# A decoder layer on one core: the order of the block products in the second MLP product, and where the final norm's row work stands on ScalarE

## The chip, the core and the metric

The kernel runs on one core of a Trainium2 chip, in one launch. The metric is the device time of one execution in microseconds (us), lower is better. The core has a matrix engine (TensorE, in the profile PE for the matmuls and PEld for its weight loads), a vector engine (VectorE, DVE), a scalar engine (ScalarE, ACT), GpSimd (POOL) and a sync engine (SyncE, SP) that here only issues transfers. Each engine works through its own instructions in the order in which they were written, and an instruction that has to wait holds up all that stand behind it on its engine.

## The reference, cut to what matters

The layer is a mixer with two head groups, a cross-attention, a squared-ReLU MLP and a final norm, over 512 tokens of width 1024. The change lies in the last two lines, in the second MLP product (4096 x 1024) and the final norm:

```
x = x + cross_attention(rms_norm(x, norm_xattn), rms_norm(mem, norm_mem), ...)
h = rms_norm(x, norm_mlp)
x = x + jnp.square(jax.nn.relu(h @ w_ff1)) @ w_ff2
return rms_norm(x, norm_final)

def rms_norm(x, g):
    y = x * lax.rsqrt(jnp.mean(x * x, axis=-1, keepdims=True) + NORM_EPS)
    return y * g
```

## The kernel before

Activations lie transposed in SBUF, features on the 128 partitions and tokens along the free axis. All instructions stand in an order written out by hand (`tc.manual_schedule()`), so the order of the Python code is the order on each engine.

**Units.** All weights pass through the kernel in units of 128 x 1024 f32 (512 KB). Unit `u` is loaded by SyncE into a raw tile `wr{u}`, then split into two parts of lower precision that together hold it: ScalarE writes the high part `wh{u}` (`A.activation(..., AF.Copy)` into fp32r), VectorE writes the rest `wl{u}` (`wr - wh`). TensorE then does three matmuls for each block: high x high, high x low, low x high. `need(u)` stands ahead of unit `u`'s matmuls and writes the splits up to unit `u + 2`; there are four buffers for `wh` and three for `wl`, so a split can run only a few units ahead of TensorE.

**The second MLP product.** It is done by block products after Strassen and Winograd: seven products of quarter-size blocks instead of eight. Products 0 to 5 (`p` in the code) are computed "across" (tokens on the partitions) in eight units of 12 matmuls with 512 columns, into the PSUM pairs X, Y or Z; product 6 ends in eight units of 24 matmuls with 256 columns into W. The units of this stage are 124 to 179: position 0 has units 124 to 131, position 1 has 132 to 139, and so on; the last, product 6, has 172 to 179. Each product has four operands `op{i}`, again a high part from ScalarE and a low part from VectorE, made from the tiles `g0` to `g7` (the first MLP product's outcome) or from sums of them that VectorE makes in place (`make_sum`).

**From a product to the output.** When a product is done, its PSUM pair is copied or added to a pair of SBUF tiles `c` (`after_across`). A `turn` then transposes these on TensorE into a PSUM tile `ct`, four small matmuls, and VectorE adds `ct` to the residual `x1[h]` (`x10` and `x11` in the order's rows). Each `turn` has two halves, taken from the list `turns` one at a time behind the units `j = 2` and `j = 3` of a product. `place(h, t, b)` is a quarter of the residual: `h` picks the half of the features, `t` the half of the tokens (256 each).

**Row work.** Where a quarter of the residual is complete (`full`), `norm_part(h, t, n)` does what the final norm needs of row block `n`: on ScalarE a square into `fsq` (or `Sf`, the first time) and a copy scaled by the gain into `xg`, which is a part of the `g` tiles that is no longer needed; on VectorE the addition of the square to the sum `Sf{t}`. When the eight row blocks of a token half `t` are through, `final_half` sums `Sf` and the last square over the partitions with two matmuls (`fs`), ScalarE makes the reciprocal root (`rb`, an Ln and an Exp), VectorE multiplies four pieces of `xg` with it, and SyncE stores each of them.

Before the change, `norm_part` is called right after the addition, in the same place of the program:

```
for h, t, op, full in uses:
    d = place(h, t, b)
    getattr(V, op)(d, d, two(ps))
    if full:
        norm_part(h, t, 2 * b)
        norm_part(h, t, 2 * b + 1)
```

and the products run in the order 0, 1, 2, 3, 4, 5, 6. The quarter (0, 0) needs products 0 and 5 and so gets its addition in the midst of product 6; (1, 0) gets it in product 4, (1, 1) in product 5, (0, 1) in the last units of product 6 (`ends_last`).

Of the kernel before, what the change touches and what calls it, by code (L numbers as in the profile page):

```python
# [32 lines left out]
FF2 = MLP + 7 * 8  # L33
# [89 lines left out]
def hybrid_layer(ctx: ExitStack, tc: tile.TileContext, xT, memT, ws, vecs, consts, rots, out):  # L123
# [21 lines left out]
    def s2(dtype, name, shape=(T,)):  # L145
        if name.startswith(EARLY2):
            return ep.tile([P, *shape], dtype, tag="e2", name=name, bufs=N2E)
        return sp.tile([P, *shape], dtype, tag="s2", name=name, bufs=N2)

    def l8(dtype, name):  # L150

        n8[0] += 1
        if n8[0] % 5 < 2:
            return s8(dtype, name)
        return late[0].tile([P, 4, T], dtype, tag="l8", name=name, bufs=N8L)
# [4 lines left out]
    def acc_bank(name):  # L160
        return pacc.tile([P, T], F32, tag="acc", name=name)

    def side_bank(name):
        return pside.tile([P, T], F32, tag="ps", name=name)
# [21 lines left out]
    def two(ap):  # L186
        return ap.rearrange("p (n c) -> p n c", n=2)

    E, F = ([[f(i, j) for j in range(2)] for i in range(2)] for f in (f1_block, f2_block))
    FT = [[dram.tile([4, P, D], F32, name=f"u{b}_{c}") for c in range(2)] for b in range(4)]  # L190
    FU = [[t[n] for t in row for n in range(4)] for row in FT]

    def f2_across(block):

        return [block[c][:, :, 2 * T // 4 * q:2 * T // 4 * (q + 1)] for c in range(2) for q in range(4)]

    def f2_rows(i, j):

        us = [MLP + 16 * (2 * i + c) + 8 + 4 * j for c in range(2)]
        return [ws[u:u + 4] for u in us]  # L200
    XO = (0, 4, 1, 5, 2, 6, 3, 7)
    sources = [ws[u] for u in range(MLP - 8)] + [ws[MLP - 8 + n] for n in XO] + [None] * (FF2 - MLP)
    LAST = (0, 2, 1, 3)
    for block in (f2_rows(0, 0), FT[0], FT[1], f2_rows(1, 1), FT[2], f2_rows(1, 0)):
        sources += f2_across(block)
    sources += FU[3][:4] + [FU[3][4 + n] for n in LAST]

# [150 lines left out]
    def start(g, key, wait=0.0):  # L358
        rec = [g, None, key]
        made[key] = rec  # L360
        side.append(rec)
        set_wait(rec, wait)
# [35 lines left out]
    def transpose(o, i):  # L398
        PE.transpose(o, i, ident)

    def mm(o, l, r, start, stop):
        last_mm[0] = PE.matmul(o, l, r, start=start, stop=stop, skip_group_check=True)
        since[0] += 1
        if since[0] >= GAP:
            pump()
# [87 lines left out]
    for i in range(2):  # L493
        t = ep.tile([P, NT, P], F32, name=f"AT{i}")
# [6 lines left out]
    def gain(g, k):  # L501
        return vec[:, g * KT + k:g * KT + k + 1]
# [599 lines left out]
    def part(k, h):  # L1102

        return g[k][:, :, h * half:(h + 1) * half]
# [13 lines left out]
    def f1_rest():  # L1118
        while rest:
            rest.pop(0)()  # L1120

    def f1_group(j):
# [36 lines left out]
        for p, ks in steps:  # L1159
# [30 lines left out]
    OPS = [lambda k: part(k, 0), lambda k: part(k, 1), lambda k: part(k, 1), lambda k: part(k, 0),  # L1190
           lambda k: part(k, 1), lambda k: part(k + 4, 0), lambda k: part(k + 4, 1)]

    def make_sum(p, k):

        if p == 2:
            V.tensor_add(part(k, 1), part(k, 1), part(k, 0))
        elif p == 3:
            V.tensor_sub(part(k, 0), part(k, 1), part(k + 4, 0))
        elif p == 4:
            V.tensor_sub(part(k, 1), part(k, 1), part(k + 4, 1))  # L1200

    sum_state = [0]

    def need_sum(i):
        while sum_state[0] < min(28, i + 1):
            make_sum(*divmod(sum_state[0], 4))
            sum_state[0] += 1

    ops = {}
    op_state = [0]  # L1210
    def make_op():

        i = op_state[0]
        op_state[0] += 1
        need_sum(i)
        src = OPS[i // 4](i % 4)
        both = l8(F32R, f"op{i}").rearrange("p a b -> p (a b)")
        hi, lo = (x.rearrange("p (k c) -> p k c", k=4) for x in (both[:, :D], both[:, D:]))
        if i // 4 == 2:
            A.activation(hi, src, AF.Copy, scale=-1.0)  # L1220
            V.scalar_tensor_tensor(lo, src, -1.0, hi.bitcast(F32), op0=ALU.mult, op1=ALU.subtract)
        else:
            A.activation(hi, src, AF.Copy)
            V.tensor_sub(lo, src, hi.bitcast(F32))
        ops[i] = [(hi[:, k], lo[:, k]) for k in range(4)]

    def need_op(i):
        while op_state[0] < min(28, i + 1):
            make_op()
# [7 lines left out]
    def place(h, t, b):  # L1237

        return x1[h][:, 2 * b:2 * b + 2, t * half:(t + 1) * half]
# [5 lines left out]
    def xg(t, a, b):  # L1245

        return part(2 * t + a // 4, 0)[:, a % 4:b - a + a % 4]

    def norm_part(h, t, n):

        f = 4 * h + n
        d = x1[h][:, n, t * half:(t + 1) * half]
        q = Sf[t] if squares[t] == 0 else s2(F32, f"fsq{f}")
        A.activation(q[:, :half], d, AF.Square)
        A.activation(xg(t, f, f + 1), d[:, None, :], AF.Copy, scale=gain(G_FIN, f))
        squares[t] += 1
        if 1 < squares[t] < KT:
            V.tensor_add(Sf[t][:, :half], Sf[t][:, :half], q[:, :half])
        elif squares[t] == KT:
            start(final_half(t, Sf[t], q), ("fin", t))  # L1260

    def final_half(nb, S, q):

        ps = side_bank("fs")
        yield [S[:, :half]]
        smm(ps[:, :half], ones, S[:, :half], True, False)
        yield [q[:, :half]]
        smm(ps[:, :half], ones, q[:, :half], False, True)
        r = rbf[:, nb * half:(nb + 1) * half]
        rsqrt_of(r, ps[:, :half], D)  # L1270
        for eng, a, b in ((V, 0, 2), (V, 2, 4), (V, 4, 7), (V, 7, 8)):
            x = xg(nb, a, b)
            eng.tensor_mul(x, x, r[:, None, :].to_broadcast([P, b - a, half]))
            SY.dma_start(out[nb, :, a:b], x)
# [12 lines left out]
            A.activation(c[m], banks[m], AF.Copy)  # L1287
        return c

    turns = []  # L1290

    def turn(c, uses):

        def one(b):
            ps = side_bank("ct")
            for n in range(2):
                for m in range(2):
                    o = n * half + m * P
                    transpose(ps[:, o:o + P], c[m][:, (2 * b + n) * P:(2 * b + n + 1) * P])
            for h, t, op, full in uses:  # L1300
                d = place(h, t, b)
                getattr(V, op)(d, d, two(ps))
                if full:
                    norm_part(h, t, 2 * b)
                    norm_part(h, t, 2 * b + 1)
        for b in range(2):
            turns.append(lambda b=b: one(b))

# [4 lines left out]
    X, Z = ([acc_bank(f"{x}{b}") for b in range(2)] for x in "XZ")  # L1313
    Y = [side_bank(f"Y{b}") for b in range(2)]
# [18 lines left out]
    def prepare(p, j):  # L1333
        i = 4 * p + j // 2
        need_op(i + 1 + j % 2)
        need_sum(i + 3)

    PLAN = ((X, True), (Y, True), (X, False), (Y, False), (X, False), (Z, True))

    for p, (banks, begins) in enumerate(PLAN):  # L1340
        for j in range(8):
            c, q = j // 4, j % 4
            w = FF2 + 8 * p + j
            need(w)
            f1_rest()
            prepare(p, j)
            hi, lo = (x[w].rearrange("p (n k c) -> p n k c", n=4, k=2) for x in (his, los))
            for kk in range(2):
                a_hi, a_lo = ops[4 * p + j // 2][(2 * j + kk) % 4]
                w_hi, w_lo = hi[:, :, kk], lo[:, :, kk]  # L1350
                for m in range(2):
                    acc = banks[m].rearrange("p (n c) -> p n c", n=4)
                    t_hi, t_lo = a_hi[:, m * P:(m + 1) * P], a_lo[:, m * P:(m + 1) * P]
                    mm(acc, t_hi, w_hi, begins and j == 0 and kk == 0, False)
                    mm(acc, t_hi, w_lo, False, False)
                    mm(acc, t_lo, w_hi, False, j == 7 and kk == 1)
            if j in (2, 3) and turns:
                turns.pop(0)()
        after_across(p)

    X = [acc_bank(f"W{b}") for b in range(2)]
    p = 6
    for j in range(8):
        i, c, n = 8 * p + j, j // 4, j % 4
        if c:
            n = LAST[n]
        need(FF2 + i)
        f1_rest()
        need_op(4 * p + 2 * c + 1 + (0, 1, 2, 2)[j % 4])
        hi, lo = his[FF2 + i], los[FF2 + i]  # L1370
        acc = two(X[n // 2])[:, n % 2]
        for k in range(8):
            a_hi, a_lo = ops[4 * p + 2 * c + k // 4][k % 4]
            w_hi, w_lo = hi[:, k * P:(k + 1) * P], lo[:, k * P:(k + 1) * P]
            mm(acc, w_hi, a_hi, c == 0 and k == 0 and n % 2 == 0, False)
            mm(acc, w_hi, a_lo, False, False)
            mm(acc, w_lo, a_hi, False, c == 1 and k == 7)
        if j in (2, 3):
            turns.pop(0)()
        if c:  # L1380
            ends_last(X, n)
    drain(("fin", 0))
# [76 lines left out]
```

## Time and profile before

| | |
|---|---|
| median of 3 runs | 751.92 us (750.88 to 751.99) |
| the profiled execution's own time | 752.65 us |
| its span, first to last instruction | 750.9 us |
| mean granted TensorE clock | 0.994 |
| busy: PE, DVE, ACT, POOL | 730.4, 546.0, 419.9, 49.5 us |
| the stage of the change, units 124 to 179 | from 576.4 us to 741.6 us of the span |

The span is what the instructions of one profiled execution cover; that execution's own time is 1.75 us longer. A row of the timeline has the start in us from the span's beginning, the duration in us, the engine, the line (here L115 nearly everywhere, a helper that records each operation), the operation, what it writes and reads with the buffers' numbers left out, and how many instructions were merged. In brackets stands how long the engine had been idle before it, and what ended that.

### The profile page before, as it was taken

How to read it: one execution, taken by the hardware profiler on the slowest of the kernel's cores; microseconds unless marked ns; L12 is line 12 of the kernel's file. 1: busy time of each engine (PE TensorE's matmuls, PEld its weight loads, DVE VectorE, ACT ScalarE, POOL GpSimd, SP SyncE). 2: the span in 40 equal slices, each digit the busy share in tenths (PEclk: the TensorE clock that was granted, in tenths of full speed). 3: DMA queues.
4: the chain of work that ended last, by engine and by line, in shares of the span. 5: the costliest groups of instructions: out<-in, count | busy, mean ns of one | idle time of the engine just before them, and what ended most of it. 6: DMA issues, size and time to landing. Idle time of an engine off the chain costs nothing.

```text
span 750.9 us, 10919 instructions
## 1 busy us (share of the span) xinstructions
PE 730.4 (97%) x4152; PEld 635.3 (85%) x4152; DVE 546.0 (73%) x893; ACT 419.9 (56%) x642; POOL 49.5 (7%) x62
## 2 busy tenths in 40 slices
PE   6999999999999999999999999999999999999994
PEld 4888888777777998888888999999999888887793
DVE  5888554877766646666468788787879688877764
ACT  6673347344855554555365755565556556647652
POOL 1000000000011210011001011222100000000000
PEclk9999999999999999999999999999999999999997
DMA  8425334534689897369826498889986765655413
GB/s 276 143 83 168 113 113 136 166 120 141 171 206 245 207 293 283 137 134 273 284 95 142 117 264 212 217 228 217 238 219 209 212 197 183 196 182 169 155 42 112
DMA packets 62868, 136.95 MB, mean 182 GB/s; under 512 B 4544, under 2 KB 31552, under 8 KB 62176
## 3 DMA queue, kind: packets, MB, share of 16 engines
q1 hardware_dynamic: 53376, 110.64, 43.4%
q0 software_dynamic: 8960, 25.17, 18.9%
q8 instruction: 32, 0.52, 0.3%
q10 hardware_dynamic: 480, 0.45, 0.2%
q14 instruction: 20, 0.16, 0.1%
HBM read 134.15 MB, written 35.65 MB: 226 GB/s over the span
## 4 chain that ended last, share of the span: by engine, by line
PE 92%; DVE 3%; ACT 2%; DMA 1%; issue 1%; DVEq 0%; ACTq 0%
PE X L115 21%; PE Y L115 15%; PE xo L115 7%; PE mkq L115 6%; PE xq L115 6%; PE wo L115 5%; PE hg L115 3%; PE mv L115 3%; PE memv L115 3%; PE hq L115 3%; PE hi L115 3%; PE Z L115 3%; PE memk L115 2%; PE W L115 2%; PE hf L115 2%; PE xs L115 2%
## 5 line engine op out<-in xcount | busy, mean ns | idle before, releaser
L115 ACT ACTIVATE wh<-wr 128x1024 fp32r<-128x1024 f32 (+2 forms) x126 | 130.3, 1042 | 111.4 <-PE wo L115 19.6
L115 DVE TENSOR_TENSOR wl<-wr,wh 128x1024 fp32r<-128x1024 f32 (+2 forms) x126 | 151.2, 1204 | 43.9 <-ACT wh L115 34.0
L115 PE MATMUL X<-wh,op 128*128 128x512 f32 x192 | 61.0, 392 | 0.1
L212 POOL DMA_DIRECT2D u<-in_ws_dram x32 | 31.0, 968 | 329.0 <-PE hg L115 201.5
L115 PE MATMUL Y<-OS,wh 128*128 128x256 f32 x256 | 47.2, 284 | 0.2 <-ACT t L115 0.2
L115 PE MATMUL X<-OS,wh 128*128 128x256 f32 x256 | 46.5, 283 | 0.0
L115 PEld LDWEIGHTS X<-wh,op 128*128 128x128 f32 x192 | 36.1, 188 | 7.9 <-ACT wh L115 0.5
L115 PEld LDWEIGHTS Y<-OS,wh 128*128 128x128 f32 x256 | 39.9, 192 | 0.5 <-ACT t L115 0.4
L115 PEld LDWEIGHTS X<-OS,wh 128*128 128x128 f32 x256 | 39.9, 192 | 0.0
L115 PE MATMUL Y<-wh,op 128*128 128x512 f32 x128 | 39.7, 389 | 0.0
L115 PE MATMUL X<-wl,op 128*128 128x512 f32 x96 | 37.5, 391 | 0.8 <-DVE wl L115 0.8
L115 PE MATMUL X<-OS,wl 128*128 128x256 f32 x128 | 36.2, 283 | 0.0
L115 PE MATMUL Y<-OS,wl 128*128 128x256 f32 x128 | 36.2, 283 | 0.0
L115 ACT ACTIVATE g<-t 128x512 f32<-128x512 f32 x32 | 19.0, 625 | 30.5 <-DVE t L115 30.5
L115 ACT ACTIVATE op<-g 128x1024 fp32r<-128x1024 f32 x28 | 29.3, 1046 | 0.5 <-PE X L115 0.5
L115 DVE TENSOR_TENSOR op<-g,op 128x1024 fp32r<-128x1024 f32 x24 | 29.3, 1219 | 0.0
L115 ACT ACT_TABLE_LOAD x22 | 28.2, 1283 | 1.5 <-PEq L1447 1.2
L115 PEld LDWEIGHTS Y<-wh,op 128*128 128x128 f32 x128 | 24.0, 188 | 5.0
L115 PE MATMUL W<-op,wh 128*128 128x256 f32 x128 | 25.1, 296 | 2.3 <-DVE x L115 2.3
L115 PE MATMUL mkq<-xhi,wh 128*128 128x512 f32 x64 | 26.7, 417 | 0.0
L115 PE MATMUL mkq<-xlo,wh 128*128 128x512 f32 x64 | 26.6, 416 | 0.0
L115 PE MATMUL mkq<-xhi,wl 128*128 128x512 f32 x64 | 26.3, 411 | 0.0
(321 smaller groups left out, 2141.1 us busy)
## 6 DMA issues: line engine op xcount, KB each, us to landing
wr<-in_ws_dram SPq DMA_DIRECT2D x90, 512.0 KB, 4.3
u<-in_ws_dram POOLq DMA_DIRECT2D x32, 512.0 KB, 7.5
wr<-u SPq DMA_DIRECT2D x32, 512.0 KB, 4.2
u<-in_ws_dram SPq DMA_DIRECT2D x16, 512.0 KB, 3.5
u<-u SPq DMA_DIRECT2D x16, 512.0 KB, 5.3
wA<-in_ws_dram SPq DMA_DIRECT2D x8, 512.0 KB, 7.1
wD<-in_ws_dram SPq DMA_DIRECT2D x8, 512.0 KB, 6.8
wB<-in_ws_dram SPq DMA_DIRECT2D x8, 512.0 KB, 4.1
```

What stands on the lines that cost most here:

```text
L115: return f(*args, **kw)
L212: return nc.gpsimd.dma_start(dst, src, accum_op=ALU.add, max_dma_last_dim=4 * D)
```

## The change

The products run in the order 0, 5, 1, 2, 3, 4, 6 (`SEQ`): product 5, which used to be sixth, becomes the second. The loads, the operands, the sums and `PLAN` follow that order. `norm_part` is no longer called where the addition is written; a call is put on a list, and `between`, which stands behind each unit, takes two of them off the list before it takes a half of a `turn`. So a row block's ScalarE work stands one unit behind the addition that it reads. The row work of quarter (0, 0) is kept back (`held_rows`) until unit `j = 3` of product 3, which sits at position 4, since it writes into parts of `g0` and `g1` that are operands up to there. In product 6 the halves of the last `turn` stand behind `j = 1` and `j = 2` instead of 2 and 3.

```diff
-    for block in (f2_rows(0, 0), FT[0], FT[1], f2_rows(1, 1), FT[2], f2_rows(1, 0)):
+    for block in (f2_rows(0, 0), f2_rows(1, 0), FT[0], FT[1], f2_rows(1, 1), FT[2]):
...
+    SEQ = (0, 5, 1, 2, 3, 4, 6)
+
+    def make_sum(i):
+
+        p, k = SEQ[i // 4], i % 4
...
-        src = OPS[i // 4](i % 4)
+        p = SEQ[i // 4]
+        src = OPS[p](i % 4)
...
                 if full:
-                    norm_part(h, t, 2 * b)
-                    norm_part(h, t, 2 * b + 1)
+                    rows = held_rows if (h, t) == (0, 0) else norms
+                    for n in (2 * b, 2 * b + 1):
+                        rows.append(lambda n=n: norm_part(h, t, n))
...
-    PLAN = ((X, True), (Y, True), (X, False), (Y, False), (X, False), (Z, True))
-
-    for p, (banks, begins) in enumerate(PLAN):
+    PLAN = {0: (X, True), 5: (Z, True), 1: (Y, True), 2: (X, False), 3: (Y, False), 4: (X, False)}
+
+    def between(at, pos, j):
+        if (pos, j) == (4, 3):
+            norms.extend(held_rows)
+        for _ in range(2):
+            if norms:
+                norms.pop(0)()
+        if j in at and turns:
+            turns.pop(0)()
+
+    for pos, p in enumerate(SEQ[:6]):
+        banks, begins = PLAN[p]
...
-            if j in (2, 3) and turns:
-                turns.pop(0)()
+            between((2, 3), pos, j)
         after_across(p)
...
-        if j in (2, 3):
-            turns.pop(0)()
+        between((1, 2), p, j)
```

The number of instructions on each engine is the same before and after. Three places show the move.

ScalarE at position 5, units 168 to 171, where in the kernel before the quarter (1, 1) is finished. `Sf1`, `fsq` and `g3` are the row work, `wh` the units' high parts:

```order
L115 ACTIVATE wh168_6684<-wr168_6600 128x1024
L115 ACTIVATE Sf1_5785<-x11_1875 128x256
L115 ACTIVATE g3_3813<-x11_1875,vec_85 128x256
L115 ACTIVATE fsq5_6708<-x11_1875 128x256
L115 ACTIVATE g3_3813<-x11_1875,vec_85 128x256
L115 ACTIVATE wh169_6715<-wr169_6618 128x1024
L115 ACTIVATE op23_6719<-g7_3817 128x1024
L115 ACTIVATE fsq6_6740<-x11_1875 128x256
L115 ACTIVATE g3_3813<-x11_1875,vec_85 128x256
L115 ACTIVATE fsq7_6744<-x11_1875 128x256
L115 ACTIVATE g3_3813<-x11_1875,vec_85 128x256
L115 ACTIVATE wh170_6751<-wr170_6643 128x1024
```

The same units on ScalarE after the change (product 4 now, and the quarter (1, 0)):

```order
L115 ACTIVATE wh169_6706<-wr169_6617 128x1024
L115 ACTIVATE op23_6710<-g3_3813 128x1024
L115 ACTIVATE fsq4_6725<-x11_1875 128x256
L115 ACTIVATE g1_3811<-x11_1875,vec_85 128x256
L115 ACTIVATE fsq5_6729<-x11_1875 128x256
L115 ACTIVATE g1_3811<-x11_1875,vec_85 128x256
L115 ACTIVATE wh170_6741<-wr170_6640 128x1024
L115 ACTIVATE fsq6_6757<-x11_1875 128x256
L115 ACTIVATE g1_3811<-x11_1875,vec_85 128x256
L115 ACTIVATE fsq7_6761<-x11_1875 128x256
L115 ACTIVATE g1_3811<-x11_1875,vec_85 128x256
L115 ACTIVATE wh171_6766<-wr171_6659 128x1024
```

The first four pieces of row work stood ahead of `wh169` and now stand behind it; the next four stood ahead of `wh170` and now stand behind it.

VectorE in the last units of product 6 before the change. `x10<-..,W` are the last additions, `g0` and `g1` the multiplications that finish token half 0, `wl179` the last unit's low part:

```order
L115 TENSOR_TENSOR x10_1874<-x10_1874,W0_6829 128x256
L115 TENSOR_TENSOR Sf1_5785<-Sf1_5785,fsq0_7010 128x256
L115 TENSOR_TENSOR wl179_7015<-wr179_6861,wh179_7014 128x1024
L115 TENSOR_TENSOR g0_3810<-g0_3810,rb2_2241 128x2x256 x2
L115 TENSOR_TENSOR g1_3811<-g1_3811,rb2_2241 128x3x256
L115 TENSOR_TENSOR g1_3811<-g1_3811,rb2_2241 128x256
L115 TENSOR_TENSOR x10_1874<-x10_1874,W1_6830 128x256
```

After the change these multiplications stand on VectorE where product 4 ends and product 6 begins:

```order
L115 TENSOR_TENSOR wl171_6767<-wr171_6659,wh171_6766 128x1024
L115 TENSOR_TENSOR op24_6770<-g4_3814,op24_6770 128x1024
L115 TENSOR_TENSOR g0_3810<-g0_3810,rb2_2241 128x2x256 x2
L115 TENSOR_TENSOR g1_3811<-g1_3811,rb2_2241 128x3x256
L115 TENSOR_TENSOR g1_3811<-g1_3811,rb2_2241 128x256
L115 TENSOR_TENSOR wl172_6801<-wr172_6680,wh172_6800 128x1024
L115 TENSOR_TENSOR wl173_6819<-wr173_6704,wh173_6818 128x1024
L115 TENSOR_TENSOR op25_6822<-g5_3815,op25_6822 128x1024
```

They no longer stand ahead of an addition that reads W, but ahead of the low parts of units 172 and 173 and of operand 25.

SyncE after the change, where the stores of token half 0 now stand ahead of the last four loads (before, all eight of these loads stood ahead of the stores):

```order
L115 DMA wr174_6739<-u3_0_83 128x1024
L115 DMA wr175_6764<-u3_0_83 128x1024
L115 DMA out_0_dram<-g0_3810 128x2x256 x2
L115 DMA out_0_dram<-g1_3811 128x3x256
L115 DMA out_0_dram<-g1_3811 128x256
L115 DMA wr176_6798<-u3_1_84 128x1024
L115 DMA wr177_6816<-u3_1_84 128x1024
```

So the loads of units 176 to 179 are issued only after VectorE's four multiplications.

More of the change, by code (lines that the diff above doesn't have):

```diff
@@ L1191, in hybrid_layer @@
            lambda k: part(k, 1), lambda k: part(k + 4, 0), lambda k: part(k + 4, 1)]
-    def make_sum(p, k):
+    SEQ = (0, 5, 1, 2, 3, 4, 6)
+    def make_sum(i):
+        p, k = SEQ[i // 4], i % 4
         if p == 2:
@@ L1205, in need_sum @@
         while sum_state[0] < min(28, i + 1):
-            make_sum(*divmod(sum_state[0], 4))
+            make_sum(sum_state[0])
             sum_state[0] += 1
@@ L1215, in make_op @@
         need_sum(i)
-        src = OPS[i // 4](i % 4)
+        p = SEQ[i // 4]
+        src = OPS[p](i % 4)
         both = l8(F32R, f"op{i}").rearrange("p a b -> p (a b)")
         hi, lo = (x.rearrange("p (k c) -> p k c", k=4) for x in (both[:, :D], both[:, D:]))
-        if i // 4 == 2:
+        if p == 2:
             A.activation(hi, src, AF.Copy, scale=-1.0)
@@ L1288, in kept @@
         return c
-    turns = []
+    turns, norms, held_rows = [], [], []
     def turn(c, uses):
@@ L1300, in one, with use @@
             for h, t, op, full in uses:
+                use(h, t, op, full, b, ps)
+        def use(h, t, op, full, b, ps):
                 d = place(h, t, b)
@@ L1336, in prepare @@
         need_sum(i + 3)
-    PLAN = ((X, True), (Y, True), (X, False), (Y, False), (X, False), (Z, True))
-    for p, (banks, begins) in enumerate(PLAN):
+    PLAN = {0: (X, True), 5: (Z, True), 1: (Y, True), 2: (X, False), 3: (Y, False), 4: (X, False)}
[9 more added lines that the diff above has]
+        banks, begins = PLAN[p]
         for j in range(8):
-            c, q = j // 4, j % 4
-            w = FF2 + 8 * p + j
+            w = FF2 + 8 * pos + j
             need(w)
             f1_rest()
-            prepare(p, j)
+            prepare(pos, j)
             hi, lo = (x[w].rearrange("p (n k c) -> p n k c", n=4, k=2) for x in (his, los))
             for kk in range(2):
-                a_hi, a_lo = ops[4 * p + j // 2][(2 * j + kk) % 4]
+                a_hi, a_lo = ops[4 * pos + j // 2][(2 * j + kk) % 4]
                 w_hi, w_lo = hi[:, :, kk], lo[:, :, kk]
```

## The prediction

> **What bounds the kernel now.** I read the page's busy shares first, then who TensorE waits for, then the timeline around each of those waits, engine by engine, and at last the windows with the granted clock.
>
> ```profile
> PE 730.4 (97%) x4152; PEld 635.3 (85%) x4152; DVE 546.0 (73%) x893; ACT 419.9 (56%) x642; POOL 49.5 (7%) x62
> PE W L115 <- DVE x L115: 2.3, 1, 2.3
> PE Z L115 <- DVE wl L115: 0.8, 1, 0.8
> PE X L115 <- DVE wl L115: 0.8, 1, 0.8
> ```
>
> TensorE is busy for 97% of the span: only what shortens its own work or its idle time shortens the kernel. The change takes no matmul away. What is left are three waits in the second MLP product: one in X at product 4, one in Z at product 5, one in W at the end. The rows give their price, which is more than the idle time.
>
> The wait in Z, at unit 170 (PE, then ACT, then DVE; the X wait at unit 162 last):
>
> ```profile
> 704.74 0.39 PE L115 MATMUL Z<-wl,op 128*128 128x512 f32 x1
> 705.42 0.39 PE L115 MATMUL Z<-wl,op 128*128 128x512 f32 x1
> 707.37 0.50 PE L115 MATMUL Z<-wl,op 128*128 128x512 f32 x1 [0.76 <-DVE wl L115]
> 707.71 0.63 PE L115 MATMUL Z<-wh,op 128*128 128x512 f32 x2
> ...
> 703.58 0.42 ACT L115 ACTIVATE fsq<-x 128x256 f32<-128x256 f32 x1 [2.07 <-DVE x L115]
> 705.02 1.99 ACT L115 ACTIVATE wh<-wr 128x1024 fp32r<-128x1024 f32 x2
> ...
> 699.24 0.43 DVE L115 TENSOR_TENSOR Sf<-Sf,fsq 128x256 f32<-128x256 f32 x1 [1.19 <-ACT fsq L115]
> 700.59 1.23 DVE L115 TENSOR_TENSOR wl<-wr,wh 128x1024 fp32r<-128x1024 f32 x1 [0.33 <-ACT wh L115]
> 702.87 0.68 DVE L115 TENSOR_TENSOR x<-x,ct 128x512 f32<-128x512 f32 x1
> 706.09 2.36 DVE L115 TENSOR_TENSOR wl<-wr,wh 128x1024 fp32r<-128x1024 f32 x2 [0.33 <-ACT wh L115]
> ...
> 681.97 0.50 PE L115 MATMUL X<-wh,op 128*128 128x512 f32 x1
> 683.23 0.50 PE L115 MATMUL X<-wl,op 128*128 128x512 f32 x1 [0.76 <-DVE wl L115]
> ```
>
> Three matmuls of this size take 0.68 us (704.74 to 705.42), one 0.23, a unit of twelve 2.72. The reader is to see a chain that goes back and forth: ScalarE stands at `fsq`, for 2.07 us, because VectorE's addition `x` comes at 702.87; VectorE is late because it had waited for ScalarE's earlier `fsq` (1.19) and `wh` (0.33). The four pieces of row work last from 703.58 to 705.02, and only then comes `wh` of unit 170, its `wl` at 706.09, and TensorE, in the middle of the unit's first matmuls, stands. Unit 162 shows the same: 681.97 to 683.23 is 1.26 us for what takes 0.23, a loss of 1.03; the next step takes 0.34 (707.37 to 707.71), 0.11 more. So each of the two costs 1.14 us.
>
> The end (PE; then DVE and ACT; then windows with PE, PEld, DVE, ACT, POOL busy, the granted clock, DMA):
>
> ```profile
> 734.10 0.28 PE L115 MATMUL W<-op,wl 128*128 128x256 f32 x1
> 734.46 0.28 PE L115 MATMUL W<-op,wl 128*128 128x256 f32 x1
> 737.07 0.47 PE L115 MATMUL W<-op,wh 128*128 128x256 f32 x2 [2.33 <-DVE x L115]
> 738.09 0.34 PE L115 MATMUL W<-op,wl 128*128 128x256 f32 x1
> 741.23 0.41 PE L115 MATMUL W<-op,wl 128*128 128x256 f32 x1
> ...
> 734.11 2.49 DVE L115 TENSOR_TENSOR g<-g,rb 128x512 f32<-128x512 f32 x4
> 736.51 0.41 DVE L115 TENSOR_TENSOR x<-x,W 128x256 f32<-128x256 f32 x1
> ...
> 734.76:738.17 3.41, 1.10 (x9) 1.13 (x10) 2.92 (x7) 0.82 (x2) 0.00 (x0) 1.00 0.71 242
> 738.17:741.58 3.41, 3.41 (x18) 3.41 (x17) 0.43 (x1) 0.82 (x2) 0.00 (x0) 0.50 0.19 66
> 741.58:744.99 3.41, 1.22 (x5) 0.42 (x3) 1.12 (x3) 1.71 (x4) 0.00 (x0) 1.00 0.00 0
> 681.00:684.00 3.00, 2.17 (x8) 1.26 (x8) 2.08 (x3) 3.00 (x4) 0.00 (x0) 1.00 0.00 0
> ```
>
> The last unit, 179, may overwrite its half of W only when VectorE has added the other half (`x` at 736.51), and that addition stands behind the four multiplications of token half 0, 2.40 us from 734.11 on. TensorE goes on at 737.07 where it would have at 734.58 (three W matmuls take 0.36: 734.10 to 734.46), 2.49 late. From 738.17 the granted clock is 0.50 for 3.41 us: five triples take 3.14 us (738.09 to 741.23) in place of 1.80, and the last matmul ends 0.13 later (0.41 against 0.28). So this wait costs 2.49, and 1.34 and 0.13 by the clock, with 0.07 for the restart: 4.03 us.
>
> **The change part by part.** *Row work one unit behind its addition.* At position 5 after the change, `wh169` no longer stands behind the first four pieces, and these read an addition written a unit earlier. I lay it out from the start of unit 164, in us, with 2.72 a unit and an estimated 0.4 for each transposition (its four matmuls span 0.60 and overlap with the next):
>
> ```profile
> 721.35 0.60 PE L115 MATMUL ct<-ident,c 128*128 128x128 f32 x4
> 721.99 0.69 DVE L115 TENSOR_TENSOR x<-x,ct 128x512 f32<-128x512 f32 x1 [0.90 <-PE ct L115]
> 722.71 0.42 ACT L115 ACTIVATE fsq<-x 128x256 f32<-128x256 f32 x1 [5.03 <-DVE x L115]
> 709.50 2.35 DVE L115 TENSOR_TENSOR wl<-wr,wh 128x1024 fp32r<-128x1024 f32 x2
> ```
>
> From `ct` to the end of the addition are 1.33 us. The transposition behind unit 166 starts at 8.2, the addition ends at 9.5; `wl169` and the low part of operand 23 follow to 11.8 (1.14 from one to the next, 1.22 the last, as in the pair of 2.35). ScalarE does the first four pieces from 9.5 to 11.0 and `wh170` to 12.0. The second transposition starts at 11.3, its addition ends at 13.2, `wl170` at 14.4; unit 170 begins at about 17.5. The lead is 3 us where it was nothing. Then four pieces from 13.2 to 14.7, `wh171` to 15.7, `wl171` to 17.0, against 20.2 for unit 171. The wait of 1.14 does not come back here. At position 4, ScalarE gets the four and four pieces of quarter (0, 0), whose additions were written 16 units earlier, some 43 us: nothing waits, and idle time takes the 3 us. At position 5 of the old order nothing of this is left, so both waits go: 2.28 us.
>
> *Product 5 as second.* Same matmuls, loads and operands; 12 sums, two additions to `c` and two to `x` move between positions. VectorE is the engine with least room:
>
> ```profile
> 650.00:670.00 20.00, 20.00 (x90) 16.57 (x89) 18.89 (x19) 10.61 (x11) 0.00 (x0) 1.00 0.64 197
> 713.00:730.00 17.00, 17.00 (x144) 17.00 (x144) 11.26 (x14) 8.88 (x14) 0.00 (x0) 1.00 0.13 52
> wr<-in_ws_dram SPq DMA_DIRECT2D x90, 512.0 KB, 4.3
> wr<-u SPq DMA_DIRECT2D x32, 512.0 KB, 4.2
> 734.82 2.43 SPq L115 DMA_DIRECT2D out_dram<-g  x4
> ```
>
> Its fullest stretch, with sums, (650 to 670) is busy 18.89 of 20 us, and none of TensorE's waits lies there. Position 2 gets four adds more than position 1 had (2 x 0.68 and 2 x 0.64, 2.6 us in 22), with three sums there: 8 x 1.14 + 4 x 1.14 + 3 x 1.14 + 2.6 = 19.7 of 22.6 us. Cost nothing; if VectorE falls behind there, `wl` is late by the excess. In product 6 quarter (1, 1) takes the place of (0, 0), with two more additions (1.4 us); VectorE has 5.7 us idle in 17 there, so nothing. A load from the weights lands as fast (4.3) as one from the summed blocks (4.2).
>
> *Token half 0 finishes early.* Its multiplications now stand ahead of `wl172`, `wl173` and the low part of operand 25. The chain from the last `fs` matmul, in the tail of before:
>
> ```profile
> 742.60 0.70 PE L115 MATMUL fs<-fsq,ones 128*128 128x256 f32 x2 [0.50 <-ACT fsq L115]
> 743.34 0.47 ACT L115 ACTIVATE rb<-fs,eps 128x256 f32<-128x256 f32 x1 [0.39 <-PE fs L115]
> 743.85 0.42 ACT L115 ACTIVATE rb<-rb 128x256 f32<-128x256 f32 x1
> 744.29 2.50 DVE L115 TENSOR_TENSOR g<-g,rb 128x512 f32<-128x512 f32 x4 [2.19 <-ACT rb L115]
> ```
>
> Call the start of this `fs` F; it now stands between units 169 and 170. VectorE multiplies from F + 1.69, `wl172` runs from F + 4.09 to F + 5.31, `wl173` from F + 5.23, operand 25 from F + 6.37 to F + 7.59. Unit 172 begins at F + 0.34 + 2 x 2.72 = F + 5.8; its third matmul needs `wl172` at F + 6.0, lead 0.7; its 14th needs operand 25 at F + 5.8 + 13 x 0.12 = F + 7.36, and stands 0.2 to 0.3 us. The nearest row for this cost is the same pair of engines in the same units; if all is 0.3 us earlier it costs nothing, if one more operation of 1.22 us gets in between it costs 1.5. I take 0.3.
>
> *Stores ahead of loads 176 to 179.* The stores' issue begins 0.71 us after the first multiplication and takes 2.43, so SyncE comes to these loads at F + 1.69 + 3.14 = F + 4.8; unit 176 begins at F + 5.8 + 4 x 2.88 + 2 x 0.4 = F + 18.1. With 4.2 us to land, or twice that beside the stores by my estimate, and 1.0 (1.99 for two) and 1.22 for the split, 2.6 us are left. Cost nothing.
>
> *The end.* No multiplications stand ahead of the addition of W any more; `x` follows its matmul at once. TensorE isn't idle, and the clock stays: 4.03 us go. What then ends last is the same tail, last matmul, addition, square, `fs`, `rb`, four multiplications, stores, as long as now.
>
> Sum: 2.28 + 4.03 - 0.3 = 6.0 us. The profiled execution has a time of 752.65 (span 750.9), so 746.6 against it; the median of the runs is 751.92, 0.7 below it, so I forecast 745.9.
>
> **The clock, and a rule that speaks against it.** By the windows the half clock begins 3.43 us after TensorE fell idle at 734.74, and covers just the 3.41 us that follow a window in which it was busy for 1.10. The waits of 0.76 us left it at 1.00 (681 to 684). I take the idle window as the cause. The Trainium skill, "TensorE: Matmul & The Clock Gate", Part 1, says that the clock is halved after an idle window of about 3.4 us, and warns of idle gaps longer than that. By that rule taken strictly the gap here, 2.33 us, is too short and something else halved the clock; this case's window was idle for two thirds, not wholly, and the clock fell, so the trace speaks for less than a whole window being enough.
>
> **The rivals.**
> *The clock falls all the same*, with the time in the kernel or by the phase of its windows in the runs of before (their spread is 1.1 us): then 1.34 + 0.13 stay, 747.4. For it: only one such gap in the trace. Against: the exact sequence of the windows.
> *The wait moves on*: ScalarE's or VectorE's order at positions 4 to 6 stalls TensorE as often as now, 2.3 us stay, 748.2. It decides once the lead of 3 us at unit 170 or 0.7 at unit 172 is used up.
> *The order does nothing*: the waits were not of row work but of whatever fills VectorE then, 751.9. Against it stand the bracketed releasers.
> *Slower*: the loads of 176 to 179 come too late behind the stores. Unit 176 waits once a load takes more than 18.1 - 4.8 - 2.3 = 11.0 us to land; from 17 us on the gain is gone, and at 20 us the time is 745.9 + 9 = 754.9. Against it: loads of this size land in 4.2 or 4.3 us.
>
> **How the numbers follow.** Forecast 0.70, clock 0.11, moved wait 0.10, nothing 0.04, slower 0.05. The likeliest has a range of its own of 745.0 to 746.9 (operand 25 at 0 to 1.2, and 0.5 us of spread between runs below that). The range of 744.8 to 747.9 takes in the clock and the better half of the moved waits. This kernel's measurement tells 0.2%, 1.5 us, from no change: faster 0.91, same 0.04, slower 0.05.
>
> **What would show it.** TensorE's waits for `wl` at units 162 and 170 and for `x` at 179 are gone from its list; the granted clock is 1.00 until the last matmul; at most one wait of some 0.3 us, in W, for operand 25; the four `g` multiplications run some 5 us ahead of unit 172, the first stores too. I am wrong if TensorE has a new wait over 1 us at positions 4 to 6, or if a window of half clock stands ahead of the last W matmul.

## The result, and the profile after

The changed kernel takes 745.81 us (745.70 to 745.89, 4 runs) beside 751.40 for the kernel before on the same chip (750.56 to 751.99, 4 runs): a ratio of 0.9926, interval 0.9909 to 0.9943. The forecast was 745.9, the direction and the size were right. Over all of its 39 runs in this study the kernel before has a median of 751.92, the one that the forecast was made against.

The profiled execution took 745.89 us, its span is 744.1. The page's busy shares, then the list of what TensorE waited for (total, times, longest, in us):

```profile
PE 727.9 (98%) x4152; PEld 634.1 (85%) x4152; DVE 545.7 (73%) x893; ACT 420.0 (56%) x642; POOL 49.4 (7%) x62
```

```profile
PE hf L115 <- ACT wh L115: 5.8, 1, 5.8
PE nc L115 <- ACT rbm L115: 1.1, 1, 1.1
PE hf L115 <- DVE xlo L115: 0.6, 2, 0.4
PE fs L115 <- ACT fsq L115: 0.5, 1, 0.5
PE Y L115 <- ACT t L115: 0.2, 1, 0.2
PE wo L115 <- DVE mixlo L115: 0.2, 1, 0.2
```

The waits in X, Z and W are gone and no new one stands in their place in this stage; what is left lies ahead of it (the last one at 422.7 us of the span) and in the tail. The other three engines are as busy as before.

The timeline around units 169 to 172 (ACT, then DVE, then SP, then PE):

```profile
700.17 0.42 ACT L115 ACTIVATE fsq<-x 128x256 f32<-128x256 f32 x1 [1.26 <-DVE x L115]
701.61 1.04 ACT L115 ACTIVATE wh<-wr 128x1024 fp32r<-128x1024 f32 x1
...
699.46 0.68 DVE L115 TENSOR_TENSOR x<-x,ct 128x512 f32<-128x512 f32 x1
700.05 1.22 DVE L115 TENSOR_TENSOR wl<-wr,wh 128x1024 fp32r<-128x1024 f32 x1
706.29 2.50 DVE L115 TENSOR_TENSOR g<-g,rb 128x512 f32<-128x512 f32 x4 [1.25 <-ACT rb L115]
708.71 2.36 DVE L115 TENSOR_TENSOR wl<-wr,wh 128x1024 fp32r<-128x1024 f32 x2
710.98 1.22 DVE L115 TENSOR_TENSOR op<-g,op 128x1024 fp32r<-128x1024 f32 x1
...
707.01 2.47 SPq L115 DMA_DIRECT2D out_dram<-g  x4
709.53 2.01 SPq L115 DMA_DIRECT2D wr<-u  x4
...
704.95 0.58 PE L115 MATMUL X<-wh,op 128*128 128x512 f32 x1
711.93 0.28 PE L115 MATMUL W<-op,wl 128*128 128x256 f32 x1
712.05 0.59 PE L115 MATMUL W<-op,wh 128*128 128x256 f32 x2
712.48 0.28 PE L115 MATMUL W<-op,wl 128*128 128x256 f32 x1
```

ScalarE still stands at `fsq` until an addition `x` comes, but the `wl` of unit 170 follows that addition at once and ends at 701.27; the unit's first matmul is at 704.95, a lead of 3.7 us where it was nothing. The four `g` multiplications run from 706.29, and behind them come `wl172`, `wl173` and operand 25. That operand ends at 712.20. The pair of matmuls at 712.05 takes 0.59 in place of 0.40. This stall of 0.19 us is the only one that the new order brings to TensorE in this stage; the `fs` matmuls of token half 0 have moved to an earlier place too.

The end (PE and DVE), and the windows of the clock there (columns as before: PE, PEld, DVE, ACT, POOL busy, granted clock, DMA):

```profile
731.82 0.40 PE L115 MATMUL W<-op,wh 128*128 128x256 f32 x2
734.58 0.28 PE L115 MATMUL W<-op,wl 128*128 128x256 f32 x1
...
732.02 0.42 DVE L115 TENSOR_TENSOR x<-x,W 128x256 f32<-128x256 f32 x1 [1.04 <-PE W L115]
734.90 0.42 DVE L115 TENSOR_TENSOR x<-x,W 128x256 f32<-128x256 f32 x1 [1.55 <-PE W L115]
```

```profile
734.44:737.85 3.41, 1.55 (x8) 0.75 (x6) 0.76 (x2) 1.70 (x4) 0.00 (x0) 1.00 0.00 0
737.85:741.26 3.41, 0.00 (x0) 0.00 (x0) 2.16 (x4) 0.00 (x0) 0.00 (x0) 0.50 0.61 209
```

Now VectorE waits for TensorE and no longer the reverse. Unit 179 starts at 731.82 instead of 737.07, the last addition at 734.90, and 9.2 us later the kernel ends, the same 9.2 as from 741.68 to 750.9 before. The clock falls only when the last matmul is done.

### The profile page after: what moved, and what is told of

It is laid out like the page before. It is cut to its first block, busy times and chain, and to the rows that moved or that the text cites. A ratio compares the mean times of both kernels' runs of the same rounds, so it can differ in the third digit from the quotient of the medians.

```text
span 744.1 us, 10913 instructions
## 1 busy us (share of the span) xinstructions
PE 727.9 (98%) x4152; PEld 634.1 (85%) x4152; DVE 545.7 (73%) x893; ACT 420.0 (56%) x642; POOL 49.4 (7%) x62
## 4 chain that ended last, share of the span: by engine, by line
PE 92%; DVE 2%; DMA 2%; ACT 1%; issue 1%; DVEq 0%; SPq 0%; ACTq 0%
PE X L115 21%; PE Y L115 15%; PE xo L115 7%; PE mkq L115 6%; PE xq L115 6%; PE wo L115 5%; PE W L115 3%; PE mv L115 3%; PE memv L115 3%; PE hq L115 3%; PE hi L115 3%; PE Z L115 3%; PE memk L115 2%; PE hf L115 2%; PE xs L115 2%; PE hg L115 1%
## 5 line engine op out<-in xcount | busy, mean ns | idle before, releaser
L115 ACT ACTIVATE t<-X 128x256 f32<-128x256 f32 x32 | 11.3, 376 | 27.5 <-PE X L115 27.4
```

The costliest lines, as they stand in the source:

```text
L115: return f(*args, **kw)
```

## The experiments

Theory: the gain is two waits of row work and one wait at the end with a half clock behind it; both parts of the change, the new order and the later row work, are needed. (A third, small part, the halves of the last `turn` one unit earlier in product 6, is kept in both of the next two runs; no run prices it alone.) Rivals: one part does all of it; the half clock has another source; the early multiplications or the stores cost something that is hidden.

**The order of the products alone.**

```diff
-                        rows.append(lambda n=n: norm_part(h, t, n))
+                        if rows is norms:
+                            norm_part(h, t, n)
+                        else:
+                            rows.append(lambda n=n: norm_part(h, t, n))
```

> The new order of the products alone: row work stands right behind its addition again (only quarter (0, 0) is still held back to position 4). My theory: the end is as in the changed kernel (the multiplications of token half 0 stay early), so the 4.03 us of the end are gained; at position 5 the chain between ScalarE and VectorE comes back, with one wait in X for the low part near unit 170 of about 1.1 us: 745.8 + 1.1 = 746.9 us (746.3 to 747.6). Rival, the order alone does everything: no such wait, 745.8. Rival, the order matters only because the row work was moved: multiplications late, or a wait at the end, 749 and more.

Measured: 748.18 us, ratio 0.9953 (0.9941 to 0.9966), 2.2 to 2.4 above the changed kernel and outside the expected range. TensorE's waits in the timeline:

```profile
705.43 0.50 PE L115 MATMUL X<-wl,op 128*128 128x512 f32 x1 [0.20 <-DVE wl L115]
713.51 0.39 PE L115 MATMUL W<-op,wh 128*128 128x256 f32 x1 [0.69 <-DVE op L115]
728.46 0.39 PE L115 MATMUL W<-op,wl 128*128 128x256 f32 x1 [0.74 <-DVE wl L115]
```

The wait near unit 170 came back, smaller than expected. What I had missed: the lateness is handed on to operand 25 at unit 172, whose lead is short, and the row work of product 6 holds up unit 177 in the same way (the last row above). Against the unit starts of the changed kernel the three places cost 0.50, 1.06 and 1.00 us. So the order alone is not enough; it does remove the end's wait and the half clock.

**The row work one unit later, without the new order**, the edit made to the kernel before. The halves of the last `turn` move forward in it as they do in the change, and `between` takes row work and turns off their lists in the same way:

```diff
-                    norm_part(h, t, 2 * b)
-                    norm_part(h, t, 2 * b + 1)
+                    for n in (2 * b, 2 * b + 1):
+                        norms.append(lambda h=h, t=t, n=n: norm_part(h, t, n))
...
-        if j in (2, 3):
-            turns.pop(0)()
+        between((1, 2), j)
```

> The old order of the products, with the row work one unit behind its addition (and the halves of the last turn behind j = 1 and 2 of product 6). My theory: the waits at units 162 and 170 go (2.28 us), while the multiplications of token half 0 stay near the end, some units earlier than before, so TensorE still waits near unit 178 or 179 by 1.3 to 2.0 us: 747.1 us if the clock stays at 1.00, 748.6 if it halves for one window. Rival, the row work alone does everything: no wait over 0.5 us in the last units, 745.8. Rival, the row work does nothing here: waits of 0.8 us at 162 and 170 remain, 750 to 751.

Measured: 746.58 us, ratio 0.9932 (0.9919 to 0.9944). The waits of 0.8 in X and Z are gone; two are left in W:

```profile
729.05 0.47 PE L115 MATMUL W<-op,wh 128*128 128x256 f32 x2 [0.63 <-DVE x L115]
732.44 0.47 PE L115 MATMUL W<-op,wh 128*128 128x256 f32 x2 [0.28 <-DVE x L115]
```

The theory's places, with a smaller price (0.91 instead of 1.3 to 2.0), so the time lies below the 747.1 expected. What I had missed is how much earlier token half 0 finishes here: its multiplications start at 726.08 instead of 734.11.

```profile
726.08 2.50 DVE L115 TENSOR_TENSOR g<-g,rb 128x512 f32<-128x512 f32 x4 [2.21 <-ACT rb L115]
```

Most of the gain comes without the new order, then, which adds the last 0.6 to 0.8. Whether token half 0 finishes earlier because of the later row work or of the halves of the last `turn`, no run tells.

**The multiplications taken off VectorE, nothing else changed.**

```diff
-        for eng, a, b in ((V, 0, 2), (V, 2, 4), (V, 4, 7), (V, 7, 8)):
+        for eng, a, b in ((PO if nb == 0 else V, a, b) for a, b in ((0, 2), (2, 4), (4, 7), (7, 8))):
```

> The kernel before, with the four multiplications of token half 0 on GpSimd in place of VectorE, and nothing else. My theory: the addition that unit 179 waits for has nothing ahead of it, so the wait of 2.49 us, its restart and the half clock all go, and the two waits at 162 and 170 stay: 751.4 - 4.0 = 747.4 us (746.9 to 748.4, where the upper end is GpSimd slowing VectorE down beside it). If the half clock belonged to the time or to something else than the idle 2.33 us, 1.47 us of it stay: 748.9. Rival, the end was not held up by these multiplications: 751.4.

Measured: 748.17 us, 3.9 below the runs of the kernel before beside it (752.04), ratio 0.9954 (0.9940 to 0.9968). The end's wait is gone, the other two stand as they were, and the clock stays at 1.00 until the last matmul is done (windows with the columns as before):

```profile
PE Z L115 <- DVE wl L115: 0.8, 1, 0.8
PE X L115 <- DVE wl L115: 0.8, 1, 0.8
...
737.89:741.30 3.41, 0.70 (x2) 0.30 (x2) 1.52 (x3) 1.43 (x4) 0.90 (x2) 1.00 0.44 154
741.30:744.72 3.42, 0.00 (x0) 0.00 (x0) 0.97 (x2) 0.00 (x0) 0.00 (x0) 0.50 0.88 307
```

This isolates the term of the end: 4.03 forecast, 3.9 measured in the times and 3.85 in the traces (161.43 us from the start of unit 124 to the last addition, 165.28 before).

**The stores off the loads' queue.**

```diff
-            SY.dma_start(out[nb, :, a:b], x)
+            (nc.gpsimd if nb == 0 else SY).dma_start(out[nb, :, a:b], x)
```

> The changed kernel with the four stores of token half 0 issued from GpSimd's queue, so that the loads of units 176 to 179 no longer stand behind them on SyncE. My theory, these loads had time to spare: 745.8 us, within 0.3; the loads are issued some 2.5 us earlier. Rival, loads behind stores cost something that the waits don't show: faster by 0.5 us or more.

Measured: 745.41 us, ratio 0.9915 (0.9901 to 0.9928): 0.4 below the changed kernel, a little more than the 0.3 of the theory and less than the rival's 0.5. The trace decides. The load of unit 176 is issued at 701.13 instead of 709.53, that of 177 at 703.77 instead of 710.18, and TensorE doesn't notice: from the first matmul of unit 124 to that of unit 179 it takes 155.67 us in both kernels. The loads behind the stores cost nothing. The 0.4 by which the medians differ lies in front of this stretch (0.17) and in the tail, which is 0.26 shorter (8.96 us from the last addition to the end instead of 9.22). The trace's semaphore records show where the tail gains: once the last store has landed, SyncE still passes five semaphore waits of some 0.06 us each in the changed kernel, and one here.

**The changed kernel again, as the control for the next three.**

> The changed kernel unaltered, run beside the next three on the same chip so that they can be compared within some tenths of a microsecond. My theory: 745.8 us within 0.4, and its runs lie within 0.5 us of each other, since no idle gap of over 1 us is left ahead of the last matmul that could bring the clock down in some runs only; the runs of the kernel before spread over 1.5 to 2 us. Rival, the spread of before has another source: both spread alike.

Measured: 746.00 us (745.77 to 746.07), ratio 0.9925 (0.9913 to 0.9938). Its runs lie within 0.3 us, those of the kernel before beside them between 750.51 and 752.58. Not all spread is the clock's: other kernels without such a gap spread over up to 0.9 us (744.80 to 745.69 in the last experiment).

**The multiplications late again, in the new order.** They are kept on a list and written in product 6 ahead of unit 177's addition:

```diff
+        if j == 5:
+            for f in late_out:
+                f()
         if c:
             ends_last(X, n)
```

> The changed kernel with the four multiplications of token half 0 (and their stores) put back near the end, behind the low part of unit 179 and ahead of the addition of W that unit 179 waits for. My theory: by the changed kernel's rows the multiplications end at about 732.1 us of the span and the addition at 732.5, where unit 179 would start at 731.82: a wait of 0.7 us and no half clock; operand 25 no longer stalls (0.2 less): 746.3 us (746.0 to 746.8). Rival, what counted at the end was not the place of these multiplications: no wait in W, 745.6. Rival, any wait there brings the clock down: 747.8.

Measured: 746.36 us (746.11 to 746.47), 0.36 above the control; the clock stays at 1.00.

```profile
732.33 0.47 PE L115 MATMUL W<-op,wh 128*128 128x256 f32 x2 [0.64 <-DVE x L115]
```

As the theory said. The place of these multiplications makes the wait; its price in this order is small because they start earlier against unit 179: about 2 us ahead of its undisturbed start, where it was 0.5 before (734.11 against 734.58).

**The same, each of these multiplications done twice.**

```diff
+            if nb == 0:
+                spare = s8(F32, f"spare{a}")
+                V.tensor_mul(spare[:, :b - a, :half], x, r[:, None, :].to_broadcast([P, b - a, half]))
             V.tensor_mul(x, x, r[:, None, :].to_broadcast([P, b - a, half]))
```

> As the one above, and each of the four multiplications is done a second time into a spare tile that nobody reads (work added, none left out), 2.4 us more on VectorE. My theory: TensorE stands in W ahead of unit 179 for 3.1 us, 748.7 us where the clock stays; an idle time of 3.1 us leaves between 1.5 and 3.1 us of one window of 3.41 us idle, by where the windows fall, so the clock halves for one window in part or all of the runs, 1.3 to 1.5 us more: 750.1 in those. Rival, only an idle time over a whole window halves the clock: all runs at 748.7, granted clock 1.00 up to the last matmul. Rival, the wait does not grow with VectorE's work: 746.3.

Measured: 750.94 us (750.45 to 751.51, 11 runs), 4.6 above the single ones. The eight multiplications take VectorE 5.39 us where the four took 2.49, so 2.9 us were added and not the 2.4 that I had planned. The wait is 3.55, 2.91 longer: it grows by just this work. A window of half clock follows (below), worth 1.4 us in the trace. Without it the time would be 746.36 + 2.9 = 749.3, and no run is near that. The gap came out longer than a window of 3.41 us, so its length alone says nothing against the rival of a whole idle window; the windows do, since none of them is idle throughout.

**GpSimd as a helper.** Each piece is multiplied on the engine, and stored from the queue, that its tuple names:

```diff
+        if nb == 0:
+            pieces = ((PO, q, 0, 2), (PO, q, 2, 4), (PO, q, 4, 7), (PO, q, 7, 8))
+        else:
+            pieces = ((V, SY, 0, 2), (V, nc.scalar, 2, 4), (PO, nc.scalar, 6, 8), (V, SY, 4, 6))
...
```

> The changed kernel with the multiplications of token half 0 and their stores on GpSimd and its queue, and in the tail the multiplication of two of the eight row blocks on GpSimd beside VectorE, with two of the four stores issued from ScalarE's queue. My theory: VectorE has 2.5 us less to do ahead of unit 172, the small stall at operand 25 goes (0.2), the tail's multiplications and store issues end 0.6 us earlier: 745.0 us (744.6 to 745.5). Rival, GpSimd and VectorE hold each other up when they work at the same time (beside GpSimd an addition of the sum of squares took 0.61 and 0.63 us instead of 0.43 in the run with the multiplications on GpSimd): the tail gains nothing or loses, 745.6 to 746.5.

Measured: 748.11 us, 2.1 above the control: slower, and by more than the rival had it. VectorE and GpSimd in the timeline, and TensorE's wait:

```profile
707.18 3.90 DVE L115 TENSOR_TENSOR wl<-wr,wh 128x1024 fp32r<-128x1024 f32 x2 [2.20 <-ACT wh L115]
711.00 3.00 DVE L115 TENSOR_TENSOR op<-g,op 128x1024 fp32r<-128x1024 f32 x1
...
708.67 1.31 POOL L115 TENSOR_TENSOR g<-g,rb 128x512 f32<-128x512 f32 x1
711.06 1.85 POOL L115 TENSOR_TENSOR g<-g,rb 128x768 f32<-128x768 f32 x1
...
714.05 0.39 PE L115 MATMUL W<-op,wh 128*128 128x256 f32 x1 [1.79 <-DVE op L115]
```

The low part of operand 25 takes 3.00 us instead of 1.22, 1.78 more beside a GpSimd instruction of 1.85; the pair of low parts takes 3.90 instead of 2.36. At operand 25 that is nearly the whole length of the GpSimd instruction added, not a share of it. The Trainium skill, "SBUF — State Buffer", Who interferes with whom, says that a VectorE instruction with two SBUF inputs contends with a GpSimd instruction that reads SBUF, and that the later one is fully blocked. The rows here agree on the blocking; which of the two came first they don't tell, as the starts lie 0.06 us apart (711.00 and 711.06). In the run with the multiplications on GpSimd at the end only two additions of squares took 0.2 us longer (0.61 and 0.63 instead of 0.43), as VectorE had little to do there and nobody waited.

The tail, the other half of this edit, lost too: 9.75 us from the last addition to the end instead of 9.22. In the traces unit 172 costs 1.87 more than in the changed kernel and the tail 0.53.

**The multiplications doubled where they now stand.** The added lines are those of the run with the multiplications done twice, here with one spare tile for all four.

> The changed kernel, each of the four multiplications of token half 0 done a second time into a spare tile that nobody reads (work added, none left out), where they stand now, ahead of the low parts of units 172 and 173 and of operand 25. My theory: 2.4 us more there use up the lead of 0.7 at unit 172: TensorE waits 1.5 us for the low part of unit 172 and then about 0.8 for operand 25, 746.0 + 2.4 = 748.4 us where the clock stays; the two gaps leave about 2.4 us of a window of 3.41 us idle, so in most runs the clock halves for one window, 749.8. Rival, VectorE has room there: 746.0. Rival, two gaps of under 2 us each don't bring the clock down: 748.4 in all runs.

Measured: 749.29 us, its runs at 748.25 and at 749.15, 749.42 and 749.59. TensorE's waits in the profiled execution (749.59):

```profile
712.28 0.39 PE L115 MATMUL W<-op,wl 128*128 128x256 f32 x1 [1.87 <-DVE wl L115]
714.55 0.58 PE L115 MATMUL W<-op,wh 128*128 128x256 f32 x1 [0.70 <-DVE op L115]
```

One run lies at the theory's 748.4, the other three (median 749.42) near its 749.8, and both places are right. Here too 2.9 us were added (5.41 instead of 2.50). In the changed kernel the low part of unit 172 has a lead of 0.9 us (it ends at 709.93, the unit's third matmul starts at 710.85) and operand 25 has none. From unit 124 to unit 179 the trace is 4.29 us longer: the 2.9 in full, and what is left, 1.4, is the half clock. So this is the place from which the moved work would have cost.

**The kernel before, twice more for its clock.**

> The kernel before once more, for one profile. Its runs so far lie in two groups, 750.5 to 751.2 and 751.6 to 752.6 us. My theory: the idle 2.33 us at unit 179 fall into windows of 3.41 us whose edges stand differently in each run; where over half of one window (1.7 us) is idle, the next has the half clock and the run is in the upper group; where the gap is shared by two windows more evenly, the clock stays at 1.00 up to the last matmul and the run is in the lower group. So either a half-clock window ahead of the last W matmul with a time over 751.5, or none with a time below 751.3. Rival, the groups have another source: a half-clock window in a run of the lower group, or none in one of the upper.

> The kernel before a further time, for a second profile with another position of the windows. The same: a half-clock window ahead of the last W matmul and a time over 751.5 us, or none and a time below 751.3.

Measured: 750.39 us, and 751.96: one of each group. Both wait 2.33 at unit 179:

```profile
736.26 0.47 PE L115 MATMUL W<-op,wh 128*128 128x256 f32 x2 [2.33 <-DVE x L115]
```

```profile
736.64 0.47 PE L115 MATMUL W<-op,wh 128*128 128x256 f32 x2 [2.33 <-DVE x L115]
```

The changes of the granted clock stand on a grid of 3.41 us, which lies elsewhere in each execution; laid back from them, these are the windows around the idle time (first number behind the comma: TensorE busy; the clock is the 1.00 or 0.50). First the run of 750.39:

```profile
731.25:734.66 3.41, 2.68 (x23) 2.48 (x21) 2.51 (x4) 1.64 (x3) 0.00 (x0) 1.00 0.01 2
734.66:738.07 3.41, 1.81 (x15) 1.84 (x16) 2.44 (x6) 1.51 (x4) 0.00 (x0) 1.00 0.91 308
738.07:741.48 3.41, 2.43 (x15) 1.62 (x14) 0.61 (x2) 1.36 (x4) 0.00 (x0) 1.00 0.00 0
```

The run of 751.96:

```profile
734.70:738.11 3.41, 1.47 (x12) 1.50 (x13) 2.55 (x6) 1.17 (x4) 0.00 (x0) 1.00 0.82 279
738.11:741.52 3.41, 3.41 (x16) 2.94 (x14) 0.85 (x2) 0.57 (x3) 0.00 (x0) 0.50 0.08 29
```

The kernel with doubled multiplications at unit 172:

```profile
710.92:714.33 3.41, 1.57 (x11) 1.37 (x11) 3.41 (x4) 2.73 (x3) 0.00 (x0) 1.00 0.88 296
714.33:717.74 3.41, 3.19 (x15) 3.19 (x16) 1.68 (x3) 0.65 (x1) 0.00 (x0) 0.50 1.01 346
```

And the one with them doubled at the end:

```profile
729.41:732.82 3.41, 2.06 (x18) 1.85 (x16) 3.31 (x6) 0.00 (x0) 0.00 (x0) 1.00 0.22 77
732.82:736.23 3.41, 1.22 (x10) 1.25 (x11) 2.77 (x6) 0.91 (x3) 0.00 (x0) 1.00 0.65 229
736.23:739.64 3.41, 3.41 (x17) 3.39 (x16) 0.54 (x2) 0.73 (x2) 0.00 (x0) 0.50 0.00 1
```

A window in which TensorE is busy for 1.10 (the profile of before), 1.22, 1.47 or 1.57 us is followed by the half clock; one with 1.81 or 2.06 is not. The bound lies between 1.57 and 1.81 of 3.41 us, about one half, and two gaps in a window add up (in the kernel with doubled multiplications at unit 172 the wait of 1.87, of which 1.36 inside the window, and 0.48 of the second). With the grid laid over all fourteen profiles there is no exception: behind the clock's first rise, every window with 1.57 us busy or less is followed by the half clock, and none with 1.81 or more.

**Spread over product 6, stores from GpSimd's queue.**

```diff
         between((1, 2), p, j)
+        if 1 <= j <= 4:
+            pieces.pop(0)()
```

> The changed kernel with the four multiplications of token half 0 spread over product 6, one each behind units 173 to 176, and their stores issued from GpSimd's queue. My theory: operand 25 no longer stands behind them, its stall of 0.2 us goes, and nothing else waits, since the low parts of units 174 to 179 have 2 to 5 us of lead: 745.2 us (744.9 to 745.6), 0.2 below the run with only the stores moved. Rival, the pieces make x<-W late again near unit 178: a wait there of 0.3 to 0.6, 745.9.

Measured: 745.09 us (744.80 to 745.69), ratio 0.9914 (0.9900 to 0.9927), the fastest of all. The stretch from unit 124 to unit 179 takes 155.49, 0.18 less than in the changed kernel: the stall at operand 25 is gone, and TensorE has no wait in W. Of the rest of the 0.7 to 0.9 below the changed kernel, 0.25 lies in the tail (8.97 us, as in the other run with the stores on GpSimd's queue) and about 0.36 in front of unit 124. The two intervals overlap; that the spreading itself gains is shown by the trace for 0.18 us, not by the runs.

## Why the prediction was right

The trace gives 6.53 us from the start of unit 124 to the last addition of W (576.40 to 741.68 before, 165.28; 576.15 to 734.90 after, 158.75), beside a forecast sum of 6.0. By its steps, from the unit starts of both traces:

*The two waits of row work: 2.28 forecast, 2.78 measured* (1.38 and 1.40). This term was mis-sized. It began at the unit's first matmul and so missed that this one was late too; before the change the row just ahead of the wait shows it:

```profile
704.97 0.61 PE L115 MATMUL Z<-wh,op 128*128 128x512 f32 x2
705.65 0.96 PE L115 MATMUL Z<-wh,op 128*128 128x512 f32 x2
```

The second matmul of this pair is unit 170's first and waits for `wh`: the pair takes 0.96 in place of 0.61, of which 0.23 is a later start. No idle row stands there: the first matmul of the pair is busy until 706.04, the second starts at 706.11, and the view merges the two. The mechanism was right: the first experiment brings waits back at units 170, 172 and 177, the second removes those at 162 and 170 without the new order. The forecast lead of 3 us at unit 170 was 3.7.

*The end: 4.03 forecast; 2.48 for the wait and 1.53 for the half clock measured, 4.01.* GpSimd in VectorE's place removed 3.9, with the other waits left as they were.

*The half clock.* The idle window was the cause, as I took it; the rival that the clock falls all the same is out. But it was taken as fixed: it is paid in about two thirds of the runs of the kernel before (25 of 39 by their times, median 752.22; the other 14 have 750.70; two of the 39 and the execution shown before were profiled, and all three fit). A gap of 2.33 us on a grid of 3.41 with its bound at one half should do it in (3.41 - 2.33 + 2 x (2.33 - 1.71)) / 3.41 = 68% of the positions, an estimate from these rows (60% to 74% with the bound anywhere between 1.57 and 1.81 busy); 64% were seen. The profiled execution and the median of the runs shown both lay in the upper group, so subtracting the whole term was right for the median, and the gain against a run of the lower group is 4.8 to 4.9 us only. The prediction weighed a rule of the Trainium skill, "TensorE: Matmul & The Clock Gate", Part 1: an idle window, or gaps longer than about 3.4 us. The windows measured here differ from it and decide: 1.94 idle us of one gap (1.47 busy), or 1.84 of two (1.57 busy), were enough.

*Operand 25: 0.3 forecast, 0.18 to 0.19 measured;* the lead at unit 172 was forecast at 0.7 and is 0.9. The four multiplications run 4.3 us ahead of unit 172 (706.29 to 710.62), where some 5 were forecast. *Product 5 as second, the rows at position 4, the stores ahead of the loads: 0 forecast, 0 measured;* the last by its own experiment. *The tail: 9.2 us both times.* The `fs` matmuls of token half 0 (two pairs), which I had not counted as moved, cost 0.95 at unit 169 and 0.85 less at 177.

So 2.78 + 4.01 - 0.18 - 0.10 = 6.51, which is the trace's 6.53. Against the profiled execution of before the forecast was 746.6, and the changed kernel's has 745.89: 0.5 of the difference are the waits, 0.25 an earlier start of unit 124. Against the median the forecast of 745.9 is closer, because the profiled execution of before lay 0.7 above its median and that of after lies at its own. That the median was met to 0.1 us is therefore in part luck: the 0.76 us that the forecast fell short of between the two profiled executions and the 0.73 taken off for the median cancel. *The moved wait* would have come at unit 172, as the prediction named it, and costs 3.3 us there once the multiplications are doubled; *the order does nothing* and *slower by late loads* are out.

## What to carry to other kernels

Look for what stands ahead of an addition that frees PSUM for the last units: work that could run elsewhere for 0.2 us cost 2.48 there, its whole length, and with the half clock 4.0; how much of its length is paid depends on how late it starts (0.64 in the new order). Put work that reads another engine's result a step behind that result, so that the two queues don't answer each other in turns, and check the next place with a short lead, since a stall that is left over is handed on to it. Where runs of one kernel fall into two groups, look at the clock's windows in a profile of each: the same gap can leave the clock alone in one run and halve it in the next.

## What was not expected of the hardware

- A half clock needs no idle window of 3.41 us: over about one half of a window is enough (busy 1.57 us or less: halved; 1.81 or more: not), in several gaps together, and by the position of the grid the same gap of 2.33 us costs 1.5 us more in one run and nothing more in the next.
- A GpSimd multiplication that reads SBUF held up a VectorE instruction with two SBUF inputs for almost its own length: 3.00 us instead of 1.22 beside 1.85.
- GpSimd's multiplications took 5.60 us for what VectorE does in 2.49 (in the run with them on GpSimd at the end, where VectorE worked beside them).
